# Attention maxima of two heads in one step: 64-row matmuls side by side, one maximum for two PSUM banks, float16 transposition

## The chip, the cores and the metric

One core of a Trainium2 chip. The metric is the time of one execution on the device in microseconds, the median of the runs shown. The core's engines are named as the profile names them: PE (TensorE, matrix products), PEld (its weight loads), DVE (VectorE), ACT (ScalarE), POOL (GpSimd) and SP (SyncE, here the queue that issues most DMAs). PE writes its results to PSUM banks; DVE and ACT read them, POOL works in SBUF alone.

## What is computed

One layer of a model on 2048 tokens of width 1024 with 256 context tokens: a modulated norm, one input projection, retention (four heads of 128) and grouped attention beside each other, an output projection, and a squared-ReLU MLP of width 4096. The change touches the attention, which is cut from the reference here:

```python
ATT_HEADS = 8; ATT_KV_HEADS = 2; ATT_GROUP = 4; ATT_HD = 64; Q_BLOCK = 128

def _dense_attention(q, k, v):
    s = jnp.einsum('bqkgd,bskd->bkgqs', q, k).astype(jnp.float32) * ATT_SCALE
    p = jax.nn.softmax(s, axis=-1).astype(v.dtype)
    return jnp.einsum('bkgqs,bskd->bqkgd', p, v)
```

2048 queries in 16 blocks of 128, two key heads with four query heads each, 64 dimensions, and 2304 keys (256 of the context, 2048 of the sequence).

## The kernel before

The program has three stages. The projections (to about 680 us of the profile) make queries, keys, values and the retention's inputs. The attention stage (to about 1640 us) runs attention with retention, the output projection and the preparation of the MLP beside it. The MLP takes the rest.

**Numbers as parts.** The float32 operands are split into a high and a low float16 part. Keys lie in `ks`: rows 0 to 63 the high part of the 64 dimensions, rows 64 to 127 the low part. Queries of one group lie in `qr`, a tile of 128 rows with two planes x four heads x 128 queries. Plane 0 has the high part twice, in rows 0 to 63 and 64 to 127, so that one matmul with `ks` gives high x high + low x high. Plane 1 has the low part in rows 0 to 63, and in rows 64 and up the rows that subtract each query's greatest score. Its partner is `ks2`: a copy of the high keys in rows 0 to 63 and constants (`unit`) in the others.

**Groups and slots.** A group is one query block and one key head: 32 groups, in the order of `order`. Time is cut into slots; in each slot every piece of work registered with `on(slot, phase, function)` is issued, phase by phase in the order of `PHASES` (begin, scores, piece, maximum, early, exp, cast, low, chain, pe, values, late, dma). Each engine runs its instructions in that order. A `chain` holds small steps that are issued one at a time after the phases maximum, low and late; `settle` forces them.

Group n takes 18 slots for its maxima from slot k = 18 n on, and from 22 slots (`LAG`) later 18 slots for its scores. So in each slot stand the scores of one group and the maxima of the next:

- `load`: four DMAs bring the queries (14 slots ahead).
- `piece(i)`: PE multiplies one head's queries with 512 keys by all 128 rows, into one of two PSUM banks tagged `mp`; one slot a piece, nine pieces for two heads, as the last 256 keys of two heads share one.
- `maximum(i)`, a slot later: DVE takes the negated maximum of that bank into `nm`.
- `least`, slot k + 18: DVE takes the least of the five values of each head, twice, into columns 64 and 96 of the float32 tile `mt`, which is otherwise zero but for a constant column 80.
- `turn`, slot k + 19: PE transposes the four heads' `mt` into another `mp` bank.
- `rows`, slot k + 20: ACT writes rows 64 and up, scaled, to plane 1 of `qr`; `rows2`, slot k + 21: DVE writes what float16 left over to rows 96 and up.
- `scores(kt)`: two matmuls of 512 columns (`ks` with plane 0, `ks2` with plane 1) into one of two banks `st`; `exp` on ACT a slot later; every second slot `cast` on ACT makes the high float16 part of two key tiles; `low` makes the low part, on POOL as one instruction of 1024 elements for the pairs in `POOL_PAIRS`, else on DVE as two of 512; `values` on PE multiplies both parts with the values in 16 small matmuls.

The first group's maxima are taken in the projection stage. Retention (`score`, `head`, `product`, all fp32 matmuls), transpositions and the output projection's products stand in the phase "pe", in a cycle of 35 slots for each block of 128 rows.

`more_keys` makes `ks2` in six steps, from slot 18 on; `first_maximum`, in the projections, uses `piece` and `maximum` with other pools.

Of the kernel before, what the change touches and what calls it, by code (L numbers as in the profile page):

```python
# [11 lines left out]
F32 = mybir.dt.float32  # L12
F32R = mybir.dt.float32r
F16 = mybir.dt.float16
BF16 = mybir.dt.bfloat16
I32 = mybir.dt.int32
AF = mybir.ActivationFunctionType
ALU = mybir.AluOpType
AX = mybir.AxisListType
# [3 lines left out]
P = 128  # L23
# [6 lines left out]
NK = NT + NC  # L30
H = 4
CH = 128
HD = 64
# [3 lines left out]
PSHIFT = 8  # L37

ROW = 8192.0
VW = 2 * HD + 1  # L40
POOL_PAIRS = (0, 2, 4, 6, 7)

C_RQ, C_RK, C_RV, C_RG, C_AQ, C_AKV = 0, 512, 1024, 1536, 2048, 2560

# [5 lines left out]
def bc(ap, shape):  # L50
    return ap.to_broadcast(shape)
# [3 lines left out]
def layer_kernel(ctx: ExitStack, tc: tile.TileContext, a: dict, out: bass.AP):  # L55
    nc = tc.nc
    mm = nc.tensor.matmul

    const = ctx.enter_context(tc.tile_pool(name="const", bufs=1, reuse_waits="tile"))
    dram = ctx.enter_context(tc.tile_pool(name="dram", bufs=1, space=DRAM))  # L60

    ident = const.tile([P, P], F32, name="ident")
    make_identity(nc, ident)

    def split(hi, lo, src, eng=None):
        nc.scalar.activation(hi, src, AF.Copy)
# [64 lines left out]
    ks = kp.tile([P, 2, NK * P], F16, name="ks")  # L131
# [9 lines left out]
    class Group:  # L141
# [7 lines left out]
        def load(self, pool=None, tag="qr", bufs=4):  # L149
            self.qr = (pool or qp).tile([P, 2, 4, P], F16, name="qr", tag=tag, bufs=bufs)  # L150
            q = self.qr.rearrange("p x (j e) t -> p x j e t", e=2)
            for e in range(2):
                src = aq_d[self.t][64 * e : 64 * e + 64, :, 2 * self.g : 2 * self.g + 2]
                nc.sync.dma_start(q[:64, :, :, e], src)
                nc.sync.dma_start(q[64:, 0, :, e], src[:, 0])

        def minima(self, pool):
            self.nm = pool.tile([P, 2, 2, 5], F32, name="nm", tag="nm")
# [12 lines left out]
        def maximum(self, i):  # L171
# [5 lines left out]
                src, dst = m.rearrange("p (e k) -> p e k", e=2), self.nm[:, h, :, 4]  # L177
            nc.vector.tensor_reduce(dst, src, axis=AX.X, op=ALU.max, negate=True)  # L178

        def least(self, mt):  # L180
            self.mt = mt
            nm = self.nm.rearrange("p a b c -> p (a b) c")
            for c in (64, 96):
                nc.vector.tensor_reduce(mt[:, :, c], nm, axis=AX.X, op=ALU.min)

        def turn(self):
            self.m = psS.tile([P, 4, P], F32, name="mp", tag="mp")
            for h in range(4):
                nc.tensor.transpose(self.m[:, h], self.mt[:, h], ident)

        def rows(self):
            nc.scalar.activation(self.qr[64:, 1], self.m[64:], AF.Copy, scale=1 / ROW)

        def rows2(self):
            lo = self.qr[96:, 1]
            nc.vector.scalar_tensor_tensor(lo, self.m[96:], 1 / ROW, lo, op0=ALU.mult, op1=ALU.subtract)

        def scores(self, kt):
            ps = self.s[kt] = psS.tile([P, 512], F32, name="st", tag="st")
# [60 lines left out]
    with ExitStack() as st:  # L260
# [628 lines left out]
        maxima = weight_maxima()  # L889
# [74 lines left out]

    ks2 = vp.tile([P, 2, NK * P], F16, name="ks2")
    unit = vp.tile([P, 1], F32, name="unit")
    nc.vector.tensor_tensor(unit, ident[:, 64:65], ident[:, 96:97], op=ALU.add)
    nc.vector.tensor_tensor(unit, unit, ident[:, 80:81], op=ALU.add)
    nc.vector.tensor_scalar_mul(unit, unit, ROW)
    zeros = vp.tile([P, P], F16, name="zeros")  # L970
    nc.vector.memset(zeros, 0.0)
    mts = [vp.tile([P, 4, P], F32, name=f"mt{i}") for i in range(2)]
    for mt in mts:
        nc.gpsimd.memset(mt, 0.0)

        nc.gpsimd.memset(mt[:, :, 80], PSHIFT * math.log(2.0) * HD**0.5)

    def more_keys(g, i):
        s = slice(i * 768, (i + 1) * 768)
        nc.scalar.activation(ks2[:64, g, s], ks[:64, g, s], AF.Copy)  # L980
        nc.vector.tensor_copy(ks2[64:, g, s], bc(unit[64:], [64, 768]))

    def bank(i, shape=(P, 4, P)):
        return psX.tile(list(shape), F32, name=f"bank{i}", tag=f"bank{i}")
# [3 lines left out]
    def on(k, phase, fn, *args):  # L988
        events.setdefault((k, phase), []).append((fn, args))
# [12 lines left out]
    def settle(what):  # L1002
        while what not in settled:
            link()
# [13 lines left out]
    def attention():  # L1018
        for n, g in enumerate(groups):
            k = NK * n  # L1020
            if n > 0:
                on(k - 14, "dma", g.load)
                on(k - 1, "late", g.minima, sm)
                for i in range(NK):
                    on(k + i, "piece", g.piece, i)
                    on(k + i + 1, "maximum", g.maximum, i)
            else:
                on(k + NK, "begin", g.load)
            on(k + NK, "chain", g.least, mts[n % 2])
            on(k + NK + 1, "piece", g.turn)  # L1030
            on(k + NK + 2, "cast", g.rows)
            on(k + NK + 3, "early", g.rows2)
            k += LAG
            for i in range(NK):
                on(k + i, "scores", g.scores, i)
                on(k + i + 1, "exp", g.exp, i)
            for j in range(NK // 2):
                on(k + 2 * j + 3, "cast", g.cast, j)
                if j in POOL_PAIRS:
                    on(k + 2 * j + 4, "low", g.low, j)  # L1040
                else:
                    for i in range(2):
                        on(k + 2 * j + 4 + i, "low", g.low, j, i)
                on(k + 2 * j + 6, "values", g.values, j)
            k += NK + 5
            on(k, "cast", g.evacuate)
            on(k + 1, "chain", g.invert)
            on(k + 2, "late", g.combine, ats)
        return NK * len(groups) + LAG + 8
# [758 lines left out]
```

## Time and profile before

| | |
|---|---|
| median of three runs | 2942.91 us (2938.74 to 2949.07) |
| profiled execution | 2946.76 us, its span 2945.0 us |
| granted PE clock | 0.987 |
| PE busy | 2776.2 us (94%) |
| DVE busy | 2181.6 us (74%) |
| ACT busy | 1388.0 us (47%) |
| POOL busy | 1550.2 us (53%) |

A row of a group reads: line of the kernel, engine, operation, output and inputs by the program's names, shapes and type, count, then busy time in us and the mean of one in ns, then the idle time of the engine just before them and who ended it. A row of the order of time has start, length, engine, line and operation. A matmul's shape begins with the rows and columns of the array that it uses (128*128 is all of it). A matmul's end is modelled, some 0.17 us behind the moment at which the next can start, so starts are compared, and a short wait can be hidden in a busy PE. Slices are fortieths of the span, their digits tenths.

### The profile page before, as it was taken

To read this page: it belongs to the slowest core of one execution; us is meant where nothing else is said; L and a number is where in the kernel's file an instruction comes from. 1 tells how busy PE (TensorE), PEld (TensorE's weight loads), DVE (VectorE), ACT (ScalarE), POOL (GpSimd) and SP (SyncE) were. 2 spreads that over 40 slices of the span, in tenths; PEclk is the share of its full clock that TensorE was granted. 3 is DMA by queue.
4 is the path that set the end of the run, shared out by engine and by line. 5 is a ranking of instruction groups with operands and counts; after the bars stand their busy time and mean duration, and the time that the engine had idled before them with its cause. 6 is when DMAs were issued, how large, how long until landed. Compare 5 with 4: busy or idle time off the path is not lost. (4 is left out here: it accounts for less than half of the span.)

```text
span 2945.0 us, 45295 instructions
## 1 busy us (share of the span) xinstructions
PE 2776.2 (94%) x17140; PEld 1648.8 (56%) x17140; DVE 2181.6 (74%) x3330; ACT 1388.0 (47%) x2280; POOL 1550.2 (53%) x1274
## 2 busy tenths in 40 slices
PE   7998898998799999999999899999999899999998
PEld 3777677775566666565666444444444344444443
DVE  5889847647987777777876577778777777777776
ACT  2333323325777777787777433333332333333332
POOL 3536326425876667887656656664443444444332
PEclk9999999999999999999999999999999999999999
DMA  9988843426412123332211723331114511111111
GB/s 300 340 283 280 271 154 107 160 67 201 137 46 81 49 63 121 90 104 85 73 63 51 273 92 101 104 102 60 53 51 154 173 60 47 54 51 51 58 44 58
DMA packets 265305, 346.95 MB, mean 118 GB/s; under 512 B 106231, under 2 KB 163831, under 8 KB 263294
## 3 DMA queue, kind: packets, MB, share of 16 engines
q1 hardware_dynamic: 254806, 336.57, 35.2%
q10 hardware_dynamic: 10280, 7.48, 0.9%
q8 instruction: 135, 2.21, 0.3%
q14 instruction: 84, 0.69, 0.1%
HBM read 272.52 MB, written 71.46 MB: 117 GB/s over the span
## 5 line engine op out<-in xcount | busy, mean ns | idle before, releaser
L178 DVE TENSOR_REDUCE nm<-mp 128x1 f32<-128x512 f32 (+1 forms) x576 | 390.9, 685 | 172.6 <-PE mp L165 143.3
L219 POOL TENSOR_TENSOR plo<-p,phi 128x1024 f16<-128x1024 f32 x160 | 353.7, 2212 | 172.9 <-ACT phi L212 139.6
L208 ACT ACTIVATE p<-st 128x512 f32<-128x512 f32 x576 | 338.1, 597 | 188.5 <-PE st L203 118.7
L1582 PE MATMUL pd<-w2hi,uhi 128*128 128x512 f16 x1024 | 388.0, 379 | 12.9 <-DVE acc L1585 12.6
L1583 PE MATMUL pd<-w2lo,uhi 128*128 128x512 f16 x1024 | 388.0, 379 | 0.6 <-DVE w2lo L71 0.6
L1584 PE MATMUL pd<-w2hi,ulo 128*128 128x512 f16 x1024 | 388.1, 379 | 0.0
L1585 DVE SCALAR_TENSOR_TENSOR acc<-pd,sc,acc 128x512 f32<-128x512 f32 x512 | 366.4, 739 | 5.7 <-PE pd L1584 5.6
L1522 PE MATMUL pu<-hf,w1f 128*128 128x512 f16 x896 | 340.1, 380 | 2.5 <-DVE q L1545 2.0
L1523 PE MATMUL pu<-hf,w1f 128*128 128x512 f16 x896 | 340.0, 379 | 0.0
L1524 PE MATMUL pu<-hf,w1f 128*128 128x512 f16 x896 | 339.8, 379 | 0.0
L824 PE MATMUL pso<-whi,hi_l 128*128 128x512 f32 (+1 forms) x768 | 295.8, 388 | 10.2 <-ACT xs L524 4.3
L212 ACT ACTIVATE phi<-p 128x1024 f16<-128x1024 f32 x288 | 303.8, 1055 | 0.0
L826 PE MATMUL pso<-whi,lo_l 128*128 128x512 f32 (+1 forms) x768 | 293.7, 383 | 4.1 <-DVE lo_l L67 4.1
L825 PE MATMUL pso<-wlo,hi_l 128*128 128x512 f32 (+1 forms) x768 | 292.9, 382 | 0.8 <-DVE wlo L67 0.7
L235 PE MATMUL o<-wv,plo 128*128 128x65 f16 x2304 | 235.9, 193 | 23.9 <-POOL plo L219 17.0
L221 DVE TENSOR_TENSOR plo<-p,phi 128x512 f16<-128x512 f32 x256 | 240.9, 942 | 18.6 <-ACT phi L212 15.7
L236 PE MATMUL o<-wv,phi 128*128 128x129 f16 x2304 | 243.8, 221 | 0.0
L235 PEld LDWEIGHTS <-plo 128*128 128x128 f16 x2304 | 206.7, 98 | 59.8 <-POOL plo L219 25.9
L202 PE MATMUL st<-qr,ks 128*128 128x512 f16 x576 | 220.2, 382 | 12.4 <-ACT p L208 10.4
L1534 POOL TENSOR_TENSOR r<-r 128x512 f32<-128x512 f32 x64 | 66.3, 1039 | 295.2 <-ACT r L1533 295.2
L203 PE MATMUL st<-qr,ks 128*128 128x512 f16 x576 | 220.0, 382 | 0.1
L165 PE MATMUL mp<-ks,qr 128*128 128x512 f16 x512 | 196.7, 384 | 23.0 <-DVE nm L178 22.2
(324 smaller groups left out, 5751.4 us busy)
## 6 DMA issues: line engine op xcount, KB each, us to landing
wm<-in_w_ff SPq DMA_DIRECT2D x64, 512.0 KB, 5.3
w1r<-in_w_ff SPq DMA_DIRECT2D x64, 512.0 KB, 4.6
ws<-in_w_ff SPq DMA_DIRECT2D x124, 256.0 KB, 3.5
wst<-in_w_in SPq DMA_DIRECT2D x60, 512.0 KB, 5.5
wst<-in_w_mod SPq DMA_DIRECT2D x32, 512.0 KB, 6.0
hf<-hp SPq DMA_DIRECT2D x56, 256.0 KB, 3.2
hf<-hf SPq DMA_DIRECT2D x14, 1024.0 KB, 7.1
orv<-rv SPq DMA_DIRECT2D x35, 256.0 KB, 4.0
```

Source lines behind the costliest of these rows:

```text
L178: nc.vector.tensor_reduce(dst, src, axis=AX.X, op=ALU.max, negate=True)
L208: nc.scalar.activation(self.p[kt // 2][:, kt % 2], self.s.pop(kt), AF.Exp, scale=HD**-0.5)
L212: nc.scalar.activation(hi, self.p[j], AF.Copy)
L219: nc.gpsimd.tensor_tensor(lo, p, hi, op=ALU.subtract)
L235: mm(o[:, : HD + 1], lo[:, i, c], v[:, : HD + 1], start=False, stop=False)
L1522: mm(pu[i], whi, hi, start=k == 0, stop=False)
L1523: mm(pu[i], whi, lo, start=False, stop=False)
L1524: mm(pu[i], wlo, hi, start=False, stop=k == 3)
L1582: mm(ps, uh, wh, start=f == 0, stop=False)
L1583: mm(ps, uh, wl, start=False, stop=False)
L1584: mm(ps, ul, wh, start=False, stop=f == NF - 1)
L1585: nc.vector.scalar_tensor_tensor(acc[:, c], ps, sc2, acc[:, c], op0=ALU.mult, op1=ALU.add)
```

## The change

Queries: rows swap places, so that the high and the low part lie in rows 64 to 127 of planes 0 and 1, the high part again in rows 0 to 63 of plane 0, and the maxima's rows in rows 0 to 63 of plane 1. `ks2` swaps its halves accordingly: the copy of the high keys is in its rows 64 to 127.

Maxima: `pair(r)` issues, every second slot, the piece r of two heads as two matmuls of 64 rows each: one head's high queries with the high keys in rows 0 to 63, the other's with the copy in `ks2` in rows 64 to 127, into the two banks of one tile (`apart`). The low part of the keys no longer enters the maxima there. For group 1, whose copy isn't made yet, both matmuls use all 128 rows. The tile `mp` has two banks and one buffer. `maxima(r)`, a slot later, is one DVE instruction over both banks.

Least values: one reduction and two small DVE steps, in the chain, write the maximum and its remainder as float16 to columns 0 and 32 of `mt`. `turn` (slot k + 19, phase late) is four float16 matmuls with a float16 identity, into one bank of the tile `mp`; `rows` (slot k + 20, phase piece, ahead of that slot's pair) copies 64 rows with ACT; `rows2` is gone.

Low parts: the key pair 7 leaves `POOL_PAIRS`, so its low part is made by DVE in two instructions.

```diff
@@ -38,7 +38,7 @@
 
 ROW = 8192.0
 VW = 2 * HD + 1
-POOL_PAIRS = (0, 2, 4, 6, 7)
+POOL_PAIRS = (0, 2, 4, 6)
 
 C_RQ, C_RK, C_RV, C_RG, C_AQ, C_AKV = 0, 512, 1024, 1536, 2048, 2560
 
@@ -61,6 +61,8 @@
 
     ident = const.tile([P, P], F32, name="ident")
     make_identity(nc, ident)
+    ident16 = const.tile([P, P], F16, name="ident16")
+    nc.vector.tensor_copy(ident16, ident)
 
     def split(hi, lo, src, eng=None):
         nc.scalar.activation(hi, src, AF.Copy)
@@ -151,8 +153,8 @@
             q = self.qr.rearrange("p x (j e) t -> p x j e t", e=2)
             for e in range(2):
                 src = aq_d[self.t][64 * e : 64 * e + 64, :, 2 * self.g : 2 * self.g + 2]
-                nc.sync.dma_start(q[:64, :, :, e], src)
-                nc.sync.dma_start(q[64:, 0, :, e], src[:, 0])
+                nc.sync.dma_start(q[64:, :, :, e], src)
+                nc.sync.dma_start(q[:64, 0, :, e], src[:, 0])
 
         def minima(self, pool):
             self.nm = pool.tile([P, 2, 2, 5], F32, name="nm", tag="nm")
@@ -177,23 +179,47 @@
                 src, dst = m.rearrange("p (e k) -> p e k", e=2), self.nm[:, h, :, 4]
             nc.vector.tensor_reduce(dst, src, axis=AX.X, op=ALU.max, negate=True)
 
+        def pair(self, r, apart):
+
+            m = self.m[r] = psS.tile([P, 2, 512], F32, name="mp", tag="mp", bufs=1)
+            halves = (slice(0, 64), slice(64, P)) if apart else (slice(0, P),) * 2
+            for e in (0, 1) if r == 8 else (r // 4,):
+                c = slice(2048, NK * P) if r == 8 else slice(r % 4 * 512, (r % 4 + 1) * 512)
+                to = slice(256 * e, 256 * e + 256) if r == 8 else slice(0, 512)
+                for i, rows in enumerate(halves):
+                    k = (ks, ks2 if apart else ks)[i]
+                    mm(m[:, i, to], self.qr[rows, 0, 2 * i + e], k[rows, self.g, c], start=True, stop=True)
+
+        def maxima(self, r):
+            m = self.m.pop(r)
+            if r < 8:
+                src, dst = m, self.nm[:, :, r // 4, r % 4]
+            else:
+                src, dst = m.rearrange("p a (e k) -> p a e k", e=2), self.nm[:, :, :, 4]
+            nc.vector.tensor_reduce(dst, src, axis=AX.X, op=ALU.max, negate=True)
+
         def least(self, mt):
+
             self.mt = mt
+            m = sm.tile([P, 4], F32, name="least", tag="least")
             nm = self.nm.rearrange("p a b c -> p (a b) c")
-            for c in (64, 96):
-                nc.vector.tensor_reduce(mt[:, :, c], nm, axis=AX.X, op=ALU.min)
+            chain.append(lambda: nc.vector.tensor_reduce(m, nm, axis=AX.X, op=ALU.min))
+            chain.append(lambda: nc.vector.tensor_scalar_mul(mt[:, :, 0], m, 1 / ROW))
+            chain.append(
+                lambda: nc.vector.scalar_tensor_tensor(
+                    mt[:, :, 32], m, 1 / ROW, mt[:, :, 0], op0=ALU.mult, op1=ALU.subtract
+                )
+            )
+            chain.append(lambda: settled.add(("least", self.n)))
 
         def turn(self):
-            self.m = psS.tile([P, 4, P], F32, name="mp", tag="mp")
+            settle(("least", self.n))
+            self.m = psS.tile([P, 2, 512], F32, name="mp", tag="mp", bufs=1)[:, 0]
             for h in range(4):
-                nc.tensor.transpose(self.m[:, h], self.mt[:, h], ident)
+                mm(self.m[:, h * P : (h + 1) * P], self.mt[:, h], ident16, start=True, stop=True)
 
         def rows(self):
-            nc.scalar.activation(self.qr[64:, 1], self.m[64:], AF.Copy, scale=1 / ROW)
-
-        def rows2(self):
-            lo = self.qr[96:, 1]
-            nc.vector.scalar_tensor_tensor(lo, self.m[96:], 1 / ROW, lo, op0=ALU.mult, op1=ALU.subtract)
+            nc.scalar.activation(self.qr[:64, 1].rearrange("p h t -> p (h t)"), self.m[:64], AF.Copy)
 
         def scores(self, kt):
             ps = self.s[kt] = psS.tile([P, 512], F32, name="st", tag="st")
@@ -964,21 +990,21 @@
 
     ks2 = vp.tile([P, 2, NK * P], F16, name="ks2")
     unit = vp.tile([P, 1], F32, name="unit")
-    nc.vector.tensor_tensor(unit, ident[:, 64:65], ident[:, 96:97], op=ALU.add)
-    nc.vector.tensor_tensor(unit, unit, ident[:, 80:81], op=ALU.add)
+    nc.vector.tensor_tensor(unit, ident[:, 0:1], ident[:, 16:17], op=ALU.add)
+    nc.vector.tensor_tensor(unit, unit, ident[:, 32:33], op=ALU.add)
     nc.vector.tensor_scalar_mul(unit, unit, ROW)
     zeros = vp.tile([P, P], F16, name="zeros")
     nc.vector.memset(zeros, 0.0)
-    mts = [vp.tile([P, 4, P], F32, name=f"mt{i}") for i in range(2)]
+    mts = [vp.tile([P, 4, P], F16, name=f"mt{i}") for i in range(2)]
     for mt in mts:
         nc.gpsimd.memset(mt, 0.0)
 
-        nc.gpsimd.memset(mt[:, :, 80], PSHIFT * math.log(2.0) * HD**0.5)
+        nc.gpsimd.memset(mt[:, :, 16], PSHIFT * math.log(2.0) * HD**0.5 / ROW)
 
     def more_keys(g, i):
         s = slice(i * 768, (i + 1) * 768)
-        nc.scalar.activation(ks2[:64, g, s], ks[:64, g, s], AF.Copy)
-        nc.vector.tensor_copy(ks2[64:, g, s], bc(unit[64:], [64, 768]))
+        nc.scalar.activation(ks2[64:, g, s], ks[:64, g, s], AF.Copy)
+        nc.vector.tensor_scalar(ks2[:64, g, s], ks[:64, g, s], 0.0, unit[:64], op0=ALU.mult, op1=ALU.add)
 
     def bank(i, shape=(P, 4, P)):
         return psX.tile(list(shape), F32, name=f"bank{i}", tag=f"bank{i}")
@@ -1021,15 +1047,15 @@
             if n > 0:
                 on(k - 14, "dma", g.load)
                 on(k - 1, "late", g.minima, sm)
-                for i in range(NK):
-                    on(k + i, "piece", g.piece, i)
-                    on(k + i + 1, "maximum", g.maximum, i)
+                for i in range(NK // 2):
+
+                    on(k + 2 * i, "piece", g.pair, i, n > 1)
+                    on(k + 2 * i + 1, "maximum", g.maxima, i)
             else:
                 on(k + NK, "begin", g.load)
-            on(k + NK, "chain", g.least, mts[n % 2])
-            on(k + NK + 1, "piece", g.turn)
-            on(k + NK + 2, "cast", g.rows)
-            on(k + NK + 3, "early", g.rows2)
+            on(k + NK, "maximum" if n else "begin", g.least, mts[n % 2])
+            on(k + NK + 1, "late", g.turn)
+            on(k + NK + 2, "piece", g.rows)
             k += LAG
             for i in range(NK):
                 on(k + i, "scores", g.scores, i)
```

## The prediction

> **What bounds the kernel now.** I read the page first (busy shares, then the 40 slices), then the table by stage for the attention stretch, the waits of TensorE in it, and last the order of time around single matmuls, because the change is about fractions of a microsecond on TensorE, repeated some 270 times.
>
> ```profile
> PE 2776.2 (94%) x17140; PEld 1648.8 (56%) x17140; DVE 2181.6 (74%) x3330; ACT 1388.0 (47%) x2280; POOL 1550.2 (53%) x1274
> PE   7998898998799999999999899999999899999998
> DVE  5889847647987777777876577778777777777776
> POOL 3536326425876667887656656664443444444332
> ...
> L178 DVE TENSOR_REDUCE nm<-mp 128x1 f32<-128x512 f32 (+1 forms) x576 | 390.9, 685 | 172.6 <-PE mp L165 143.3
> L219 POOL TENSOR_TENSOR plo<-p,phi 128x1024 f16<-128x1024 f32 x160 | 353.7, 2212 | 172.9 <-ACT phi L212 139.6
> L221 DVE TENSOR_TENSOR plo<-p,phi 128x512 f16<-128x512 f32 x256 | 240.9, 942 | 18.6 <-ACT phi L212 15.7
> ```
>
> ```profile
> 720.00:832.00 112.00, 90.10 (x876) 63.18 (x875) 101.27 (x177) 80.92 (x131) 90.32 (x61) 0.97 0.47 149
> 832.00:1602.00 770.00, 728.02 (x6750) 476.09 (x6750) 600.53 (x1052) 583.57 (x955) 531.74 (x400) 1.00 0.25 76
> ```
>
> In the second fence the columns are length, then busy time of PE, PEld, DVE, ACT, POOL. The changed maxima (group 2 on) run from 720 to 1602 us. Until 832 the kernel is bound by DVE (101 of 112 us, PE 90); from there by PE, 728 of 770 us. So PE's time is what counts for 26 groups of 30 us, and DVE's for the four before. What PE waits for in the long stretch:
>
> ```profile
> PE o L235 <- POOL plo L219: 14.5, 10, 2.5
> ...
> PE mp L165 <- DVE nm L178: 5.4, 17, 0.7
> PE o L235 <- DVE plo L221: 4.7, 10, 1.0
> PE st L202 <- ACT p L208: 4.1, 9, 0.9
> ```
>
> All of DVE's and POOL's work in the change is worth at most these few microseconds there. The rest depends on what the paired matmuls cost PE.
>
> **Pairs on PE.** Before, each key piece of each head is one whole-array matmul; back to back they start 0.215 us apart:
>
> ```profile
> 1000.29 0.38 PE L202 MATMUL st<-qr,ks 128*128 128x512 f16 x1
> 1000.50 0.38 PE L203 MATMUL st<-qr,ks 128*128 128x512 f16 x1
> 1000.72 0.38 PE L165 MATMUL mp<-ks,qr 128*128 128x512 f16 x1
> ```
>
> Two pieces cost 0.43 us. After, their matmuls use 64 rows each and can run side by side: 0.216 us plus a small lag. But the array goes from 128*128 to 64*128 and back around every pair, as the scores before it and the work behind it use the whole array. The trace has such switches in the projection stage:
>
> ```profile
> 53.83 0.64 PE L322 MATMUL mps<-wst,cst 128*32 128x256 f32 x8
> 365.28 0.46 PE L289 MATMUL psx<-ident,mrow 64*128 64x64 f32 x4
> 365.67 0.19 PEld L826 LDWEIGHTS pso<-whi,lo_l 128*128 128x128 f32 x1
> 412.38 0.39 PE L826 MATMUL pso<-whi,lo_l 128*128 128x512 f32 x1
> 412.70 0.14 PEld L368 LDWEIGHTS mps<-macc,ones 128*32 128x32 f32 x2 [0.35 <-issue]
> 412.70 1.04 PE L368 MATMUL mps<-macc,ones 128*32 128x512 f32 x2
> 413.68 0.50 PE L824 MATMUL pso<-whi,hi_l 128*128 128x512 f32 x1
> 414.01 0.39 PE L825 MATMUL pso<-wlo,hi_l 128*128 128x512 f32 x1
> 767.61 0.20 PE L235 MATMUL o<-wv,plo 128*128 128x65 f16 x1 [0.91 <-POOL plo L219]
> 767.72 0.19 PE L235 MATMUL o<-wv,plo 128*128 128x65 f16 x1
> ```
>
> Overlap first: the eight of L322 take 0.64 us in all though one alone takes 0.38 to 0.40, so tiles of the array do run together, here column tiles. Then the switch: L826 starts at 412.38 and streams 0.23 us, to 412.61; the next weights, of another tile shape, load only at 412.70: 0.09 us lost. The last of the four L289 starts at 365.28 + 0.46 - 0.22 = 365.52, streams 0.06 us, and whole-array weights load at 365.67: again 0.09 us. On top comes the weight load that can no longer hide: 0.11 us for fp32 (0.50 against 0.39 us at 413.68), but only 0.01 to 0.02 us for float16 (0.20 against 0.19 us, behind a wait at 767.61). So a float16 pair costs 0.09 + 0.015 in, 0.216 + 0.007, 0.09 + 0.015 out: 0.433 us against 0.432. **The overlap pays for the two switches and nothing is left.** The step of the last 256 keys (four matmuls of 0.109 us) comes out the same. Bounds for a pair: 0.22 us (no drain in float16: -0.21) and 0.65 us (drain, no overlap: +0.22); I take the middle since the drain has rows in both tile shapes and both directions. Group 1 is not split and stays as it is.
>
> [...]
>
> Where an fp32 matmul follows a pair, its weights used to load behind L165 and now lie open:
>
> ```profile
> L1113 PE MATMUL bank<-oqt,okt x120: 270/275/417, 763.7 to 1569.6; 128*128 128x128 f32 x120
> 1034.34 0.22 PE L236 MATMUL o<-wv,phi 128*128 128x129 f16 x1
> 1034.40 0.19 PE L235 MATMUL o<-wv,plo 128*128 128x65 f16 x1
> 1035.09 0.63 PE L189 MATMUL mp<-ident,mt 128*128 128x128 f32 x4
> 1035.59 0.38 PE L165 MATMUL mp<-ks,qr 128*128 128x512 f16 x1
> 1036.02 0.38 PE L203 MATMUL st<-qr,ks 128*128 128x512 f16 x1
> ...
> 1036.86 0.38 PE L165 MATMUL mp<-ks,qr 128*128 128x512 f16 x1 [0.46 <-DVE nm L178]
> L192 ACT ACTIVATE qr<-mp x32: 592/592/593, 679.4 to 1605.7; 64x512 f16<-64x512 f32 x32
> L212 ACT ACTIVATE phi<-p 128x1024 f16<-128x1024 f32 x288 | 303.8, 1055 | 0.0
> ```
>
> A late L1113 takes 0.417 us instead of 0.275. In 11 of the 35 slots of a retention chunk's cycle the "pe" phase is fp32 (one of scores, four of heads, two of products, four of transposes), so some 85 of 270 pairs are followed by one: 85 x 0.1 = **+9 us** (0 to 12).
>
> **Transposition of the maxima.** Four fp32 transposes 0.109 us apart (1035.09 to 1035.59) become four float16 matmuls; the nearest row is L236 with 129 columns, whose successor starts 0.06 us later (1034.34 to 1034.40). 4 x 0.05 = 0.2 us, times 27 groups in PE's stretch: 5.4, and the first fp32 load that no longer lies open: **-6 us**.
>
> **The group boundary.** Both heads' maxima now need both banks, so there is one such tile instead of two, and the transposition uses it too. PE's order at a boundary is: the transposition at the end of slot k+19, two scores, then the next pair, which must wait until ACT has copied the maxima out of that tile. The transposition's tail (0.17), ACT's copy (0.592, L192) and two semaphores (0.1) against two scores (0.43) leave 0.43 us idle, 30 times: **+13 us**. It is 0 if the scores run long and about 1.5 us each time if ACT has just begun a cast of 1.055 us (L212). What goes: before, the transposition held one of two buffers, and the following pieces waited for DVE at the other (1036.86). That is the wait above, 5.4 us in 17, and 17 x 0.17 that the modelled matmul ends hide: **-8 us**.
>
> **Holding the tile.** A pair comes every second slot (26 groups of 18 slots in 770 us are 1.64 us a slot, so every 3.3 us), its maximum must be read between. From a pair's end to the next stand 3.3 - 0.43 - 0.43 = 2.4 us; the maximum takes 1.2. DVE is at 78% and often a slot behind: **+3 us** (0 to 13).
>
> ```profile
> L662 DVE TENSOR_REDUCE wmx<-wm 128x1 f32<-128x1024 f32 x72 | 87.1, 1211 | 14.8 <-DMA wm<-in_w_ff 11.4 <-DMA wm<-in_w_out 3.3
> L196 DVE SCALAR_TENSOR_TENSOR qr<-mp,qr 32x512 f16<-32x512 f32 x32 | 22.3, 697 | 4.8 <-ACT qr L192 3.8
> L184 DVE TENSOR_REDUCE mt<-nm x64: 157/166/176, 660.7 to 1602.7; 128x4 f32<-128x20 f32 x64
> L981 DVE CAST ks<-unit x6: 557/557/2135, 660.2 to 703.7; 64x768 f16<-64x768 f32 x6
> ```
>
> **DVE and POOL.** Per group, 18 maxima of 0.686 become nine of 1,024 elements, at L662's 1.21 us (bounds 0.69 and 1.37): -1.4 us. L196 goes: -0.7. Two L184 become one and two small ones: +0.16. The fifth POOL pair becomes two L221: +1.4 to +1.9, by 0.69 undisturbed and the mean 0.942. DVE stays about even (-0.5 to 0 per group): **-2 us** in the four DVE-bound groups. POOL loses 2.21 us of about 20 per group. That pays where PE waits for POOL's low parts (14.5 us, and 1.7 hidden); one of five pairs goes, but queueing shrinks more than its share, so I take half: **-8 us** (0 to -16), and **+1** for one more DVE pair to wait for (4.7 us for four). Key copies: L981 keeps its size (0.56 us, between 0.3 and 0.9, six times): 0, as are the constants, the smaller clears, and the query loads, which keep number and size and only swap partition halves.
>
> Sum: 0 + 9 - 6 + 13 - 8 + 3 - 2 - 8 + 1 = +2 us on the profiled execution (2946.76 us, span 2945.0, 3.9 above the median of the three runs): **2945 us** for the median 2942.91.
>
> **Rivals.** *The switches are cheap in float16.* The drains seen all stand beside fp32 matmuls. If float16 pairs lose nothing at the switches, 270 x 0.21 = 57 us go, and the other terms leave 2888; half of it gives 2917. Against: the gap is the same for two tile shapes and stands before the weight load, which is where data types differ.
>
> *The halves overlap partly or not at all* (slower). No row shows two row tiles in flight; L322's are column tiles. It decides from 0.033 us of lag per pair on (9 us): with half of the overlap lost, 0.108 us, +29 gives 2974; wholly in turn, +58 gives 3003. For: both halves write the same 128 partitions. Against: two different banks. [...]
>
> *The boundary costs more* (slower): ACT late with the copy, or the transposition waiting for the previous maximum. At 1.5 us per boundary, 30 times, +32 us: 2977.
>
> *POOL was the real limit of the groups from 1090 to 1400* (slices of 7 and 8 tenths in POOL's row): then all 16 us of the waits for it go, 8 more than taken, and if the boundary hides behind the scores, 13 more: 2924.
>
> **How the numbers follow.** My forecast has 0.40: within it terms of +-5 us each give 2928 to 2958. Cheap switches 0.18, POOL relief 0.11, partial or no overlap 0.16, boundary 0.15. A measurement of this kernel tells about 0.3% (9 us) from nothing. Faster by more: 0.18 + 0.11 + 0.08 of the forecast's own = 0.37; within: 0.27 of the forecast's and 0.02 of the rivals' edges = 0.29; slower: 0.34. The range 2888 to 2982 reaches from cheap switches to the costly boundary and leaves out no overlap at all and gains beyond the first rival, 0.15 together.
>
> **What would show it.** The two matmuls of a pair starting within 0.02 us of each other, the weights ahead of and behind them 0.09 us after the stream before ends: right. A pair that ends 0.22 us after the score's stream without gaps: the first rival. Second halves 0.2 us late: the second. After the transposition, an ACT release of the next pair of about 0.4 us: right. The maximum at about 1.2 us, L219 128 times, and PE's waits for POOL halved. What would make the number wrong most easily is the switch price: each 0.03 us in it is 8 us.

## The result, and the profile after

Over four runs each the kernel takes 2985.35 us after the change (2981.09 to 2990.32) and 2943.22 before (2938.74 to 2949.07): ratio 1.0143, 95% interval 1.0119 to 1.0167. It is 42 us slower, just above the range of 2888 to 2982, and 40 us above the predicted 2945.

First the tables by stage, before and after: length, then busy time of PE, PEld, DVE, ACT, POOL, the granted clock, DMA. The first row of each is the attention stretch, the second all that follows.

```profile
682.00:1632.00 950.00, 878.64 (x8189) 581.55 (x8189) 750.81 (x1317) 715.32 (x1167) 667.96 (x490) 0.99 0.29 88
1632.00:2945.00 1313.00, 1277.04 (x5947) 579.88 (x5945) 961.32 (x1256) 445.92 (x725) 598.38 (x464) 0.99 0.27 88
```

```profile
679.00:1666.00 987.00, 879.89 (x8186) 534.12 (x8185) 794.77 (x1101) 709.82 (x1168) 615.95 (x459) 0.98 0.27 84
1666.00:2979.00 1313.00, 1277.59 (x5951) 579.20 (x5947) 962.61 (x1258) 446.49 (x725) 595.97 (x463) 0.99 0.27 88
```

All the loss lies in the attention stretch, 37 us longer in the profiled executions; what precedes it is 3 us shorter, and what follows takes 1313 us in both. PE's busy time there hardly moves (878.6 and 879.9). DVE's grows by 44 us, with 216 instructions fewer, and the changed maxima are not why: they cost what was predicted, 1.218 us. From the page of after, engines and three groups:

```profile
PE 2778.6 (93%) x17140; PEld 1602.2 (54%) x17140; DVE 2222.8 (75%) x3116; ACT 1383.7 (46%) x2280; POOL 1495.0 (50%) x1242
...
L199 DVE TENSOR_REDUCE nm<-mp 128x2 f32<-128x1024 f32 (+1 forms) x279 | 339.8, 1218 | 98.6 <-PE mp L191 98.1
...
L245 POOL TENSOR_TENSOR plo<-p,phi 128x1024 f16<-128x1024 f32 x128 | 291.4, 2276 | 201.4 <-ACT phi L238 173.9
...
L247 DVE TENSOR_TENSOR plo<-p,phi 128x512 f16<-128x512 f32 x320 | 310.4, 976 | 60.8 <-ACT phi L238 55.0
```

Next the waits of PE in the attention stretch of after (line waited at, releaser, us in total, times, longest):

```profile
PE mp L191 <- DVE nm L199: 19.8, 23, 2.4
PE mp L219 <- DVE nm L199: 16.4, 12, 3.3
PE o L261 <- POOL plo L245: 14.6, 12, 2.8
...
PE o L261 <- DVE plo L247: 10.8, 16, 1.7
PE mp L219 <- DVE mt L209: 8.3, 2, 5.4
PE mp L191 <- ACT qr L222: 8.2, 25, 1.2
```

L219 is the transposition. It waits 24.7 us for DVE, 14 times. Before, its counterpart L189 hardly did, by the same view of before:

```profile
PE mp L189 <- DVE mt L184: 1.5, 3, 0.7
```

Two things must be ready for it. One is the tile: the next group's first pair was written into it, and its maximum, L199, must have read it. The other is `mt`, whose last writer is L209, the third of three small DVE steps. In the 12 waits put down to L199 that maximum did end last, 0.05 us ahead of the transposition; but it stands on DVE right behind L209, and the first weight load of the transposition had, as a rule, waited for L209 (us, times):

```profile
  PEld L219: 18.2, 11
```

Here is one of the twelve in order of time:

```profile
1605.74 2.04 DVE L209 SCALAR_TENSOR_TENSOR mt<-least,mt 128x4 f16<-128x4 f32 x1
...
1607.70 1.21 DVE L199 TENSOR_REDUCE nm<-mp 128x2 f32<-128x1024 f32 x1
1607.84 0.10 PEld L219 LDWEIGHTS <-mt 128*128 128x128 f16 x1 [2.33 <-DVE mt L209]
...
1608.96 0.38 PE L219 MATMUL mp<-ident,mt 128*128 128x128 f16 x4 [3.26 <-DVE nm L199]
```

Of PE's 3.26 us, 2.1 pass before L209 ends and 1.2 behind it, while the maximum runs. Over all 14 waits some 11 of the 24.7 us lie behind the end of L209 and are the shared tile's, and 13.7 us lie before it.

**What holds the small steps.** They are L206, L207 and L209, with four results a partition each. By line and shape over the stretch (busy us, mean ns):

```profile
L209 DVE SCALAR_TENSOR_TENSOR mt<-least,mt 128x4 f16<-128x4 f32 x32 | 16.0, 499 | 0.9
L207 DVE TENSOR_SCALAR mt<-least 128x4 f16<-128x4 f32 x32 | 15.8, 492 | 0.2
L206 DVE TENSOR_REDUCE least<-nm 128x4 f32<-128x20 f32 x32 | 5.4, 168 | 0.7
```

The reduction takes 0.168 us; the two others, no larger, 0.49 to 0.50 us on average. Their shortest, median and longest (ns):

```profile
L207 DVE TENSOR_SCALAR mt<-least x32: 157/171/2046, 655.7 to 1637.5; 128x4 f16<-128x4 f32 x32
```

```profile
L209 DVE SCALAR_TENSOR_TENSOR mt<-least,mt x32: 143/177/2044, 655.9 to 1637.8; 128x4 f16<-128x4 f32 x32
```

So most take what the reduction takes, and some up to twelve times as long. One of these in order of time (start, duration in us), DVE's, POOL's and PE's rows:

```profile
1133.33 0.16 DVE L206 TENSOR_REDUCE least<-nm 128x4 f32<-128x20 f32 x1
1133.52 2.05 DVE L207 TENSOR_SCALAR mt<-least 128x4 f16<-128x4 f32 x1
1135.60 0.18 DVE L209 SCALAR_TENSOR_TENSOR mt<-least,mt 128x4 f16<-128x4 f32 x1
```

```profile
1133.42 2.11 POOL L245 TENSOR_TENSOR plo<-p,phi 128x1024 f16<-128x1024 f32 x1
```

```profile
1135.84 0.40 PE L219 MATMUL mp<-ident,mt 128*128 128x128 f16 x4 [2.88 <-DVE mt L209]
```

POOL's subtraction began 0.1 us ahead of L207 and ends at 1135.53; L207, which needs 0.17 us by itself, ends at 1135.57. PE stands idle for 2.88 us. Of the 64 executions of L207 and L209, 21 begin while a POOL instruction is under way. Eighteen of these take longer than 0.3 us, and every one of the 18 ends 0.03 to 0.04 us after the end of that POOL instruction, of seven different lines; the other three met L1035 or L1036 and were not held, which stays open. The 43 that begin with POOL idle take at most 0.18 us. The reduction beside them is not held: of the 32 L206, 17 begin with a POOL instruction under way, and none takes over 0.175 us. Why the two forms differ no run shows.

**The pairs.** Here is one in the order of time:

```profile
1017.69 0.38 PE L229 MATMUL st<-qr,ks 128*128 128x512 f16 x1
1018.00 0.10 PEld L191 LDWEIGHTS <-qr 64*128 64x128 f16 x2 [0.42 <-issue]
1018.00 0.39 PE L191 MATMUL mp<-ks,qr 64*128 64x512 f16 x2
...
1018.32 0.10 PEld L1300 LDWEIGHTS <-ah 128*128 128x128 f16 x1 [0.23 <-issue]
1018.32 0.39 PE L1300 MATMUL bank<-wo,ah 128*128 128x512 f16 x1
```

The two halves are one row, as they start 3 ns apart and take 0.39 us together, what one takes: full overlap. The score's stream ends at 1017.69 + 0.22 = 1017.91 and the pair starts at 1018.00: 0.09 us. Its own stream ends at 1018.22, the next matmul starts at 1018.32: 0.10 us. From 1017.91 to 1018.32 the pair takes 0.41 us, where two whole-array matmuls before took 0.43. The example is typical: in all 240 pairs of two matmuls the halves start 0.002 to 0.007 us apart, and the median gap is 0.096 us ahead of a pair and 0.103 us behind it.

### The profile page after: what moved, and what is told of

Its sections match the earlier page's. It is cut to its first block, busy times and chain, and to the rows that moved or that the text cites. A ratio compares the mean times of both kernels' runs of the same rounds, so it can differ in the third digit from the quotient of the medians.

```text
span 2979.3 us, 44958 instructions
## 1 busy us (share of the span) xinstructions
PE 2778.6 (93%) x17140; PEld 1602.2 (54%) x17140; DVE 2222.8 (75%) x3116; ACT 1383.7 (46%) x2280; POOL 1495.0 (50%) x1242
## 5 line engine op out<-in xcount | busy, mean ns | idle before, releaser
L199 DVE TENSOR_REDUCE nm<-mp 128x2 f32<-128x1024 f32 (+1 forms) x279 | 339.8, 1218 | 98.6 <-PE mp L191 98.1
L245 POOL TENSOR_TENSOR plo<-p,phi 128x1024 f16<-128x1024 f32 x128 | 291.4, 2276 | 201.4 <-ACT phi L238 173.9
L247 DVE TENSOR_TENSOR plo<-p,phi 128x512 f16<-128x512 f32 x320 | 310.4, 976 | 60.8 <-ACT phi L238 55.0
L262 PEld LDWEIGHTS <-phi 128*128 128x128 f16 x2304 | 207.7, 98 | 13.6 <-issue 0.3
```

The costliest lines, as they stand in the source:

```text
L247: nc.vector.tensor_tensor(lo[:, i], p[:, i], hi[:, i], op=ALU.subtract)
L262: mm(o, hi[:, i, c], v[:, :VW], start=False, stop=last)
```

## The experiments

The ratios are to the kernel before, run beside each set of kernels on the same chip (medians 2949.32, 2947.68, 2949.22 and 2947.68 us for the four sets), each with its 95% interval. The kernel after was not run again beside them, so a difference from its 1.0143 carries both intervals, and so does a difference between two sets. The edits are shown shortened, without prefixes and some keyword arguments. The four kernels of the first set each change one thing in the kernel after.

**Reductions in place of the held steps.** Least and remainder by four reductions; the scaling moves into ACT's copy.

```diff
-tensor_reduce(m, nm, op=min)
-tensor_scalar_mul(mt[:, :, 0], m, 1 / ROW)
-scalar_tensor_tensor(mt[:, :, 32], m, 1 / ROW, mt[:, :, 0], mult, subtract)
+tensor_reduce(m[:, :, 0], nm, op=min)
+tensor_reduce(mt[:, :, 0], nm, op=min)
+tensor_reduce(m[:, :, 1], mt[:, :, 0:1], op=max, negate=True)
+tensor_reduce(mt[:, :, 32], m, op=add)
```

> The changed kernel, but the least value and its float16 remainder are made by four DVE reductions (one input each) in place of one reduction, a tensor_scalar and a scalar_tensor_tensor with two inputs. Same numbers, one instruction more. Theory P (the small DVE steps wait for the POOL instruction that is under way, up to 2.05 us, and hold the maxima and the transposition behind them): all of these steps take 0.14 to 0.18 us, the 20.8 us that the two lines take beyond 0.17 us each vanish, PE's wait ahead of the transposition falls from 27.5 us to under 12, time about 2985 - 20 = 2965 (2958 to 2972). Rival T (the one two-bank tile that maxima and transposition share makes the wait): 2985 within 6. Rival S (the switches of the array's shape are what costs): 2985.

Measured: 2968.06 us, 1.0066 (1.0049 to 1.0083), as theory P expected; about half of the loss is gone, 0.0077 of 0.0143 (some 0.005 to 0.011, estimated from the two intervals). The last two of the four reductions, by line and shape:

```profile
L217 DVE TENSOR_REDUCE mt<-least 128x4 f16<-128x8 f32 x32 | 5.4, 169 | 0.9
...
L213 DVE TENSOR_REDUCE least<-mt 128x4 f32<-128x4 f16 x32 | 4.8, 151 | 0.1
```

L217 takes at most 0.174 us, the other three have means of 0.151 to 0.169 us, and the transposition (now L226) waits 11.5 us for DVE instead of 24.7:

```profile
PE mp L191 <- DVE nm L199: 19.8, 24, 2.4
...
PE mp L191 <- ACT qr L229: 11.2, 31, 1.3
PE o L268 <- DVE plo L254: 11.0, 16, 1.7
...
PE mp L226 <- DVE nm L199: 7.8, 10, 1.3
...
PE mp L226 <- DVE mt L217: 3.7, 2, 2.6
```

**The transposition in another tile.** It no longer waits for the pair's tile, nor the next pair for its copy.

```diff
-self.m = psS.tile([P, 2, 512], F32, name="mp", tag="mp", bufs=1)[:, 0]
+self.m = psS.tile([P, 512], F32, name="st", tag="st")
```

> The changed kernel, but the transposition goes to one of the two score banks, so it needn't wait for the next group's first maximum and the next pair needn't wait for ACT's copy of it. Theory P: the wait ahead of the transposition stays where the small DVE steps are late (8.6 us of it and part of the 18.9 us), the wait of the pair for ACT's copy (12 us) goes, scores wait instead for a bank: 2985 - 15 = 2970 (2962 to 2982). Rival T: both waits go, 2985 - 35 = 2950. Rival S: 2985.

Measured: 2997.55 us, 1.0169 (1.0151 to 1.0186). None of the three expectations held. The wait for ACT's copy grew and moved to the scores, which share that tile's buffers, and the small steps still hold the transposition:

```profile
PE st L228 <- ACT qr L222: 25.2, 31, 2.3
...
PE st L219 <- DVE mt L209: 13.5, 7, 5.4
```

The wait for the maximum is gone, and the 13.5 us for L209 that stay agree with the 13.7 us that passed before L209's end in the kernel after. But the time says nothing on what the boundary is worth: the kernel replaced one wait by a longer one.

**No switch at all.** Both matmuls of a pair over the whole array, in the same tile, with the same maximum.

```diff
-on(k + 2 * i, "piece", g.pair, i, n > 1)
+on(k + 2 * i, "piece", g.pair, i, False)
```

> The changed kernel, but both matmuls of every pair use all 128 rows of the array, as for group 1: no overlap, no switch of shape, low parts of the keys in the maxima again. Everything else as changed. Theory P (overlap and two drains of 0.09 us cancel, 58 us against 57): PE's nominal time in the attention stage rises by 58 us, its gaps around pairs fall by 57 and the fp32 weight loads behind pairs hide again (11 us): 2985 - 10 = 2975 (2968 to 2984). Rival S (switches cost more than the trace shows): below 2965. If the overlap were worth more than the drains: above 2990.

Measured: 2984.32 us, 1.0117 (1.0098 to 1.0136): 0.0026 below after, some 8 us, close to what the open fp32 loads were predicted to cost, but the intervals overlap and this run alone does not tell it from nothing. Row halves side by side buy nothing here.

**Both halves in the same rows**, so that they cannot overlap but the switches stay.

```diff
-halves = (slice(0, 64), slice(64, P)) if apart else ...
+halves = (slice(64, P), slice(64, P)) if apart else ...
-k = (ks, ks2 if apart else ks)[i]
+k = ks2 if apart else ks
```

> The changed kernel, but both heads of a pair use rows 64 to 127 (the copy of the high keys), so the two 64-row matmuls can't run side by side, while the switches stay. It prices the overlap alone. All theories that hold the trace for right: each pair 0.213 us longer, 270 pairs, +55 us where PE binds (the DVE-bound first groups hide some): 2985 + 50 = 3035 (3022 to 3042). If the two starts 3 ns apart were not real overlap: 2985.

Measured: 3021.13 us, 1.0243 (1.0225 to 1.0261). The pair's row in the order of time:

```profile
1025.89 0.38 PE L229 MATMUL st<-qr,ks 128*128 128x512 f16 x1
1026.20 0.60 PE L191 MATMUL mp<-ks,qr 64*128 64x512 f16 x2
1026.73 0.39 PE L1300 MATMUL bank<-wo,ah 128*128 128x512 f16 x1
```

The two take 0.60 us instead of 0.39, as they should, but the kernel loses 0.0100, 29 us, less than was expected and not the 58 of 270 pairs: PE's other waits shrink when PE is later. All its waits in the attention stretch come to 83.9 us (680 to 1702 us here), against 105.8 in the kernel after (680 to 1666 us). The overlap is real, and its price in the kernel is half of its price on PE.

In the second set the boundary, POOL's share and the float16 transposition stand by themselves. **The boundary**, on top of the four reductions: the transposition one place later, ACT's copy ahead of its cast, the second pair at the end of its slot.

```diff
-on(k + 2 * i, "piece", g.pair, i, n > 1)
+on(k + 2 * i, "late" if i == 1 else "piece", g.pair, i, n > 1)
-on(k + NK + 1, "late", g.turn)
-on(k + NK + 2, "piece", g.rows)
+on(k + NK + 2, "piece", g.turn)
+on(k + NK + 2, "cast", g.rows)
```

> The kernel with the four reductions, and besides the order at the group boundary changed: the transposition moves from the end of slot k+19 into slot k+20 behind its scores, ACT's copy behind that slot's exponential, and the second pair of the next group behind that slot's value products, so that PE has scores ahead of the transposition and some 0.7 us of value products between the copy's start and the pair. Theory (the waits at the boundary, 12 us ahead of the transposition and 15 us for ACT's copy, are on PE's path): both shrink to a few us, ratio falls by 0.005 to 0.008 from the 1.0066 of the four reductions, to about 1.000. Rival (PE's waits there only stand in for waits that come anyway): within 0.002 of 1.0066.

Measured: 2966.27 us, 1.0071 (1.0055 to 1.0087), no different from the 1.0066 that it starts from. Yet the waits it aims at do go, and others take their place:

```profile
PE mp L191 <- DVE nm L199: 21.9, 32, 2.4
...
PE o L268 <- DVE plo L254: 15.2, 21, 1.7
...
PE mp L226 <- DVE mt L217: 2.2, 2, 1.6
PE mp L191 <- ACT qr L229: 2.1, 3, 0.9
PE mp L226 <- DVE nm L199: 2.0, 4, 0.9
```

The transposition and the pair behind it wait 6.3 us in these rows instead of 22.7, while DVE's low parts and maxima are waited for 37.1 us instead of 30.8 in the kernel with four reductions. The rest comes back in smaller rows: from 680 to 1660 us all waits of PE come to 95.0 us, against 95.8. A wait taken away at the boundary comes back at other places.

**POOL's fifth pair back**, on top of the four reductions: POOL_PAIRS = (0, 2, 4, 6, 7).

> The kernel with the four reductions, but the fifth pair's low part stays on POOL as before the change. Theory P (a low part on DVE reads two SBUF inputs and waits for POOL like the small steps did, so moving the pair gained nothing): ratio within 0.003 of 1.0066, with PE's waits for POOL's low parts up and those for DVE's low parts and maxima down by as much. If POOL was a limit, as the forecast took it (8 us): 1.0093 or above. If DVE is: 1.0035 or below.

Measured: 2962.01 us, 1.0054 (1.0039 to 1.0069): 0.0012 lower, which the intervals do not tell from nothing.

**The fifth pair taken from POOL, in the kernel before**: POOL_PAIRS = (0, 2, 4, 6) and nothing else.

> The kernel before with one part of the change alone: the fifth pair's low part made by DVE. Forecast's term: -8 + 1 us, ratio 0.9976. Theory P: DVE's mean for a low part rises or stays near 0.94 to 0.98 us against 0.68 undisturbed, DVE gains 60 us of work and is late for the maxima more often: ratio 1.000 to 1.006.

Measured: 2961.98 us, 1.0052 (1.0034 to 1.007), some 15 us slower, as theory P expected. POOL's part in PE's waits falls only from 17.0 us to this:

```profile
PE o L235 <- POOL plo L219: 15.3, 12, 2.5
```

**The float16 transposition alone, in the kernel before**, its two parts by four reductions and without the DVE step L196; the pieces stay as they are.

```diff
-for c in (64, 96):
-    tensor_reduce(mt[:, :, c], nm, op=min)
+# the four reductions, into columns 64 and 96 of a float16 mt
-nc.tensor.transpose(self.m[:, h], self.mt[:, h], ident)
+mm(self.m[:, h], self.mt[:, h], ident16, start=True, stop=True)
-on(k + NK + 3, "early", g.rows2)
```

> The kernel before with the float16 transposition alone (least and remainder by four reductions, four float16 matmuls, no second writing of rows by DVE); single heads, two one-bank tiles and all five POOL pairs as before. The forecast's term of -6 us on PE, and DVE 0.4 us a group less: ratio 0.995 to 0.999.

Measured: 2947.11 us, 1.0002 (0.9993 to 1.0012): nothing gained, where a small gain was expected.

The third set undoes parts together. **Two one-bank tiles and a maximum each**, with four reductions and five POOL pairs:

```diff
-m = psS.tile([P, 2, 512], F32, name="mp", tag="mp", bufs=1)
+m = [psS.tile([P, 512], F32, name="mp", tag="mp") for _ in range(2)]
```

> The kernel with four reductions and five POOL pairs, but the two halves of a pair go to two one-bank tiles again, each read by a maximum of its own (512 elements) as before the change; the 64-row matmuls side by side and the float16 transposition stay. It undoes the merged maximum and the shared tile alone. If the shared two-bank tile holds PE (two waits at the boundary and one reading of 1.22 us): ratio from 1.0054 down to about 1.000. If the rest of the loss lies elsewhere (switches with fp32 loads behind them, 11 us, and DVE): 1.003 to 1.006; DVE gains 1.4 us a group, some 40 us of work, which makes it 1.006 or more if DVE's time is what counts.

Measured: 2959.7 us, 1.0035 (1.0023 to 1.0046), against 1.0054 with the wide tile; the intervals overlap. **No switch, four reductions, five pairs**:

> The kernel with four reductions, five POOL pairs, and whole-array matmuls in each pair (no overlap, no switch). Left of the change: merged maxima on one two-bank tile, the transposition in the same tile, float16. Drains and overlap cancel, the fp32 loads hide again: ratio 1.0054 - 0.0026 = 1.0028 (1.001 to 1.0045).

Measured: 2955.58 us, 1.0019 (1.0007 to 1.0031): against the same kernel with switches, 1.0054 (1.0039 to 1.0069), the switches cost 0.0035, some 10 us, and here the intervals do not overlap. **The same with the boundary's order of above**:

> As the one before, with the order at the group boundary changed too (transposition behind the next slot's scores, second pair behind that slot's value products). If waits at the boundary only stand in for others, as the earlier run of that order said: within 0.002 of its partner without it. If they were covered there by the switches and the fifth DVE pair: 0.003 to 0.005 lower, about 0.999.

Measured: 2954.38 us, 1.0012 (1.0 to 1.0024): again not told from its partner. **A sixth pair for POOL in the kernel before**, POOL_PAIRS = (0, 1, 3, 4, 6, 7), to see whether DVE's relief pays there:

> The kernel before with six low parts on POOL (pairs 0, 1, 3, 4, 6, 7) in place of five: the opposite of the change's move. If what a low part costs on DVE is more than its 0.68 us, since it waits for POOL, the move the other way gains what the change's move lost (1.0052): ratio 0.995 to 0.998. If POOL, at 69% of the long stretch and over 80% in some groups, is then late with its parts: 1.002 or above.

Measured: 2952.83 us, 1.0007 (0.9994 to 1.0021). Neither expectation held: no gain and no loss. PE's wait for POOL grew from 17.0 us:

```profile
PE o L235 <- POOL plo L219: 20.6, 16, 3.2
```

The last set puts the suspected steps into the kernel before, where nothing else of the change is. Their results are read by nobody; they only stand ahead of the two reductions into `mt` (L184 of the kernel before). **One reduction and the two small steps as the change has them**:

```diff
+tensor_reduce(m, nm, op=min)
+tensor_scalar_mul(spare16[:, :, 0], m, 1 / ROW)
+scalar_tensor_tensor(spare16[:, :, 32], m, 1 / ROW, spare16[:, :, 0], mult, subtract)
```

> The kernel before, with three small DVE steps added ahead of the two least reductions of each group, read by nobody: one reduction, and the changed kernel's tensor_scalar and scalar_tensor_tensor of 128x4 into a spare float16 tile. Theory P: these two wait for POOL's instruction in about a third of the groups, mean 0.5 us against 0.17, and hold the maxima and the transposition behind them: ratio 1.003 to 1.008, against the twin with reductions 0.003 or more higher. [...]

Measured: 2987.38 us, 1.013 (1.0116 to 1.0144). **The same with reductions in their place**:

```diff
+tensor_reduce(spare16[:, :, 0], nm, op=min)
+tensor_reduce(spare16[:, :, 32], spare16[:, :, 0:1], op=min)
```

> The same, but the two steps into the spare tile are reductions. Theory P: each takes 0.14 to 0.18 us and waits for nothing: 0.5 us of DVE time a group, ratio 1.000 to 1.002. [...]

Measured: 2963.4 us, 1.0053 (1.0039 to 1.0067). The rows of the two kernels, by line and shape:

```profile
L185 DVE TENSOR_SCALAR spare<-least 128x4 f16<-128x4 f32 x32 | 16.1, 503 | 1.1
L186 DVE SCALAR_TENSOR_TENSOR spare<-least,spare 128x4 f16<-128x4 f32 x32 | 16.1, 502 | 1.1
```

```profile
L186 DVE TENSOR_REDUCE spare<-spare 128x4 f16<-128x4 f16 x32 | 5.5, 171 | 1.1
...
L185 DVE TENSOR_REDUCE spare<-nm 128x4 f16<-128x20 f32 x32 | 5.3, 167 | 0.0
L184 DVE TENSOR_REDUCE least<-nm 128x4 f32<-128x20 f32 x32 | 5.2, 163 | 0.0
```

Same number of instructions, as many results, same place: 0.0077 apart, 23 us (some 0.006 to 0.010, estimated from the two intervals), for 21.4 us of DVE time (32.2 against 10.8). This agrees with the 0.0077 that separates the kernel after from the one with four reductions. Had three more steps cost the same in any form, the two would have come out alike. Both kernels lie above the ranges expected for them, and only their difference is as theory P had it: plain reductions, held by nobody, 16.0 us of DVE time in all (three of 32), cost 15.6 us of the kernel's. In these two kernels, what is put on DVE ahead of the transposition is paid in full.

## Why the prediction was wrong

Step by step, in the order in which it was made.

- **"From there by PE, 728 of 770 us … All of DVE's and POOL's work in the change is worth at most these few microseconds there."** This sentence failed. It read the waits of the kernel before as the most that DVE could matter. They are what is left over at the present timing; 16 us of DVE time added at the boundary cost 15.6 us. DVE is busy for 78% of the long stretch, and these kernels show no slack at the place where PE needs it.
- **"Two L184 become one and two small ones: +0.16."** The term that was most mis-sized. The price was that of a reduction; the three steps of the change cost 0.168 + 0.492 + 0.499 = 1.16 us a group, 0.83 more than the two L184. Over 32 groups that is 26 us, and held steps are 0.0077 of the kernel (23 us), shown twice, by removing them and by adding them to the kernel before. The warning stood in a row that the prediction quoted: L221, with two inputs, at a mean of 0.942 us against 0.69 undisturbed. It was read as a price for that shape instead of as a wait that L207 and L209 could meet too. The trace of before shows the wait: the 111 L221 that begin with no POOL instruction under way take 0.67 to 0.69 us, the 145 others up to 2.64 us, with a median of 1.00.
- **"The overlap pays for the two switches and nothing is left", +9 for fp32 loads.** Right, mechanism and size: full overlap, 0.09 to 0.10 us at each switch, and 0.0035 (10 us) back without switching where the intervals tell it from nothing. In the trace of after 78 fp32 matmuls stand right behind a pair and take 7.7 us longer in all than their like, where 85 and 9 us were forecast. The rivals "cheap switches" and "partly or not at all" both fall. The lag of 0.007 us in the sum for a pair was the author's estimate with no row beside it; the second halves start 3 ns after the first (median of the 240 pairs, 2 to 7 ns), where the second rival counts from 33 ns on. What prediction and expectations call a drain is the gap at the switch, 0.096 us ahead of a pair and 0.103 us behind it; what PE does in it no run shows.
- **The float16 transposition, -6.** True on PE, whose four matmuls there start 0.056 us apart instead of 0.109 (medians of L219 after and L189 before), but not in the kernel's time: alone with four reductions it gave 1.0002. Its two further reductions cost some 32 × 0.32 = 10 us if they cost their own time, as in the last set; that the dropped L196 and PE's gain pay for them is argued from the sums, not shown.
- **The boundary, +13 and -8.** ACT's copy does hold the next pair, 25 times, 8.2 us in the waits' view and 11.2 in the kernel with four reductions. The 0.1 us for two semaphores was an estimate; the pairs that waited start 0.05 us behind the end of the copy. But taking the wait away changed nothing, twice. It was a wait that stood in for another; as a term of a sum it was wrong. The rival "the boundary costs more" is nearest to what happened, for half of its reasons: the transposition did wait for the previous maximum in its tile, 12 times of 14, but that maximum was late itself behind the held steps, and ACT's half did not matter.
- **Holding the tile, +3 (0 to 13).** The wide tile and wide maximum against two tiles: 0.0019, 6 us, with intervals that overlap. Not contradicted.
- **POOL, -8, and +1 for DVE.** Wrong: no gain in either kernel. Alone it costs some 15 us; with the four reductions the same move makes 0.0012, which the intervals do not tell from nothing, and why the two differ is open. PE's wait for POOL fell only from 17.0 to 15.3 us although one pair of five went, and DVE got 64 subtractions more. The rival "POOL was the real limit" falls with it; the kernel before with six pairs on POOL shows that DVE's relief does not pay by itself either, and PE's waits for POOL there rise from 17.0 to 20.6 us.

Undone one after the other, the parts lead from 0.0143 to 0.0066 without held steps, 0.0054 with POOL's fifth pair and 0.0019 without the switches; the float16 transposition in the kernel before stands at 0.0002. These are steps of one chain and not prices that hold alone, as POOL's pair shows. The last difference is left open. It may be the wide maximum or the transposition's place in the order, but the kernel with two tiles and no switch was not run. None of the versions beats the kernel before.

## What to carry to other kernels

A wait in the profile is not a budget for what may be added: PE's waits for an engine show where it was late at this timing, and work added ahead of such a place can be paid in full (16.0 us of it cost 15.6 us here), while a wait taken away there may come back at the next one (22.7 us at the boundary became 6.3, and all of PE's waits went from 95.8 us to 95.0). Before a small DVE step is given a price, look at which form it is and what POOL does beside it, and read the longest as well as the median: 0.17 us and 2.05 us were the same instruction here, and reductions in the place of the held steps were worth 0.8% of the kernel. Two half-array matmuls of 512 columns between whole-array ones gained nothing here; whether several pairs in a row, sharing the two switches, would gain was not run.

## What the runs showed that was not expected

- A DVE step of four elements a partition took up to 2.05 us when POOL was in an instruction (18 of the 21 that began so were held), and ended 0.03 to 0.04 us after POOL's. Reductions with as many results, 151 to 171 ns on average, show no such hold.
- Plain reductions that nobody reads, 16.0 us of DVE time ahead of the transposition, cost 15.6 us, although PE's waits for DVE in the long stretch of the kernel before were rows of 5.4 and 4.7 us.
- Forecast from other tile shapes, and now shown: a pair's two halves, in rows 0 to 63 and 64 to 127, writing two banks, start 3 ns apart and take 0.39 us together; the same two in one set of rows take 0.60 us.
- Likewise, a switch between whole-array and half-array matmuls in float16 leaves PE without a stream for 0.09 to 0.10 us in each direction, the same as beside fp32.
